# Splitting each streamed weight tile with one ScalarE copy and one DVE subtraction over 1024 columns in place of two of each

## The chip, the cores and the metric

The kernel runs on one core of one Trainium2 chip. The metric is the device time of that core in microseconds (us). Before the change it is 2222.72 us, the median of three runs (2221.65 to 2224.61).

## What is computed

The kernel computes one layer of a decoder block on 256 tokens (S) of width 2048 (D), all in fp32. Cut to what matters:

```python
def reference(x, w_in, ..., w_branch_da, w_branch_nsa, w_out, ..., peer_wq, ..., peer_u, peer_v, ...):
    ... = split_columns(x @ w_in[l])                  # one combined projection
    o_da = diff_attention(...)                        # 8 heads
    o_nsa = nsa_attention(...)                        # compressed + selected + window
    mixed = (sigmoid(g_da_merge) * (o_da @ w_branch_da[l])
             + sigmoid(g_nsa_merge) * (o_nsa @ w_branch_nsa[l]))
    h = layer_norm(DN_ALPHA * x + mixed @ w_out[l], ...)
    x = layer_norm(DN_ALPHA * h + peer_ffn(h, peer_wq[l], ..., peer_u[l], peer_v[l]), ...)
```

`peer_ffn` forms queries `y @ w_q`, picks 16 of 128 x 128 experts for each of 8 heads by two sub-key scores, and sums `gate * gelu(u[e] . y) * v[e]` over the chosen experts. `u` and `v` have 16384 rows of 2048 values each.

## The kernel before, in words

All weights are read once from HBM, as tiles of 128 x 1024 fp32 values (512 KB), in the order in which they are used: the columns of `w_in` group by group (`CHUNKS`), the two branch weights, `w_out`, `w_q`, then all rows of `u` and all rows of `v`. The experts are not gathered: the kernel multiplies `y` with every row of `u`, keeps the scores that were picked, and multiplies the sparse result `G` with every row of `v`.

**The split.** To keep nearly fp32 accuracy, each operand is split in two rounded parts, `hi` (the value rounded to the type fp32r) and `lo` (the value minus `hi`, rounded to that type again), and each product is made of three matmuls: hi times hi, lo times hi, hi times lo. The activations are split once (`xhi`, `xlo`, later `yhi`, `ylo`, and `whi`, `wlo` for `G`). A weight tile is split when it has landed, by class `Stream` (L52 to L127): `load_to` (L74) has SP issue the load into one of three buffers named `raw`; `split_upto` (L83) has ScalarE copy a half of 512 columns into `hi` (L98) and DVE subtract it from the raw half into `lo` (L99), then does the same with the other half. There are six buffers of 512 columns for each of `hi` and `lo`, so three tiles' worth. A job of another kind ("dest", L105 and L106) writes its parts into memory of its own, with one copy and one subtraction of up to 1024 columns.

**The order.** The schedule is by hand: every engine runs its instructions in the order in which the program writes them. `step` (L156) takes the split tile of its turn, runs what earlier steps had deferred, may run some background work (attention, the pick of the experts, norms), then splits the tiles up to two ahead and issues the loads behind them (`ahead`, L118; `load_ahead`, L122), and at last writes the matmuls of its own tile. So on ScalarE and DVE the split of tile i+2 stands behind the background work of step i and ahead of that of step i+1.

**How the halves are read.** `mm_T` (L193; weights stay in the array, the 256 tokens move) and `mm_N` (L204; tokens stay, 512 weight columns move) use the first half of a tile for all its matmuls and then the second. The loop over `u` (L1235 to L1261) and the loop over `v` (L1341 to L1359, with `v_mm` at L1328) use both halves from the first matmuls on. All matmuls stand in line L191. A tile is 24 matmuls of 256 columns, or 12 of 512.

**Places that the prediction speaks of.**
- In the last groups of `w_in` `W.share` is set (L804) until the first branch product (L864): there the second half's subtraction goes to GpSimd.
- The product with `w_out` (L903 to L918) holds the last tiles in buffers of their own, so that it can be finished for tokens 0 to 127 first.
- `norm` (L928; four DVE instructions in L933) normalises half of the tokens, `y_trans` (L940) transposes them on TensorE, `y_parts` (L949) makes `yhi` and `ylo`. Ahead of this, L976 has GpSimd split the first tiles of `w_q`, for the query product that follows.
- At about 740 to 765 us GpSimd works on the rows of `h` (16 instructions at L1037) and stores them to HBM (`h_d`, L1038). Later `G` takes over the memory of that tile; the loop over `u` writes it (L1251).
- `pick` (L1103) finds the experts with long DVE instructions (`eq`, L1107; `eid`, L1111), as background work of the loop over `u`.

Of the kernel before, what the change touches and what calls it, by code (L numbers as in the profile page):

```python
# [9 lines left out]
F32 = mybir.dt.float32  # L10
F32R = mybir.dt.float32r
# [5 lines left out]
OP = mybir.AluOpType  # L17
# [7 lines left out]
HALF = 1024  # L25
# [22 lines left out]
def dap(t, offset, ap):  # L48
    return bass.AP(tensor=t.tensor, offset=t.offset + offset, ap=ap)


class Stream:  # L52
# [30 lines left out]
    def split_upto(self, n, sub=None):  # L83
        sub = sub or self.nc.vector
        while self.split_to < min(n, len(self.jobs), self.cap or n):
            i = self.split_to
            self.load_to(i + 1)
            _, width, kind, dest, _, skew = self.jobs[i]
            raw = self.raw.pop(i)
            if kind == "split":  # L90
                his, los = [], []
                nb = 1 if width <= 512 else 2
                w = width // nb
                for b in range(nb):
                    hi = self.pool.tile([128, 512], F32R, name="hi", bufs=self.nsplit)
                    lo = self.pool.tile([128, 640], F32R, name="lo", bufs=self.nsplit)[:, skew:skew + 512]
                    r = raw[:, b * w:b * w + w]
                    self.nc.scalar.copy(hi[:, :w], r)  # L98
                    (self.nc.gpsimd if self.share and b else sub).tensor_tensor(lo[:, :w], r, hi[:, :w].bitcast(F32), op=OP.subtract)  # L99
                    his.append(hi[:, :w])  # L100
                    los.append(lo[:, :w])
                self.parts[i] = (his, los)
            elif kind == "dest":
                hv, lv = dest()
                self.nc.scalar.copy(hv, raw[:, :width])  # L105
                sub.tensor_tensor(lv, raw[:, :width], hv.bitcast(F32), op=OP.subtract)  # L106
                self.parts[i] = None
            else:
                self.parts[i] = (raw,)
            self.split_to += 1  # L110
# [20 lines left out]
def block_kernel(ctx, tc, x, xT, w_in, rel_bias, onehot, lamq, lamk, subln_g, pe, w1, w2k, w2v, cmask,  # L131
                 wbda, wbnsa, wout, ln1_gT, ln1_bT, ln1_g, ln1_b, wq, subk, u, v, ln2_g, ln2_b, out):
    nc = tc.nc
# [4 lines left out]
    stream = ctx.enter_context(tc.tile_pool(name="stream", bufs=3))  # L138
# [1 line left out]
    psctx = ExitStack()  # L140
    ps = psctx.enter_context(tc.tile_pool(name="ps", bufs=1, space=PSUM))

    W = Stream(nc, stream, 3, 6)

    deferred = []
    late = []
# [3 lines left out]
    def flush(every=False):  # L150
        for q in (deferred, late) if every else (deferred,):
            for f in q:
                f()
            q.clear()

    def step(fn, credit=1.0):  # L156
        part = W.take()
        flush()
        now, late[:] = list(late), []
        state["c"] = min(state["c"] + credit, 2.0)  # L160
        post = None
        while credit and slots and state["c"] > 0 and post is None:
            cost, pre, post = slots.pop(0)
            state["c"] -= cost
            if pre:
                pre()
        for f in now:
            f()
        W.ahead()
        fn(*(part or ()))  # L170
        if post:
            post()
# [75 lines left out]
    def x_job(k, n):  # L248
        W.add(dap(xT, k * S, [[KT * S, 128], [1, n * S]]), n * S, "dest",
              lambda: [t[:, k:k + n, :].rearrange("p a b -> p (a b)") for t in (xhi, xlo)],  # L250
              xraw[:, k * S:(k + n) * S])
        plan.append(("x", None, 0, 0, n // 4))
# [4 lines left out]
    for name, form, width in CHUNKS:  # L257
        for j in range(8):
            W.skew = SKEW if form == "T" else 0
            if off == 0:  # L260
                for b in range(2):
                    x_job(b, 1)
                    W.add(dap(w_in, 512 * b, [[1024, 128], [1, 512]]), 512)
                    plan.append((name, form, width, 0, b))
                x_job(2, 2)
            else:
                if name == "qd0" and j % 2 == 0:
                    x_job(2 * j, 4)
                W.add(dap(w_in, off, [[2 * width, 128], [1, 2 * width]]), 2 * width)
                plan.append((name, form, width, j, 0))  # L270
# [509 lines left out]
    for name, form, width, j, half in plan:  # L780
# [27 lines left out]
        if form == "T":  # L808
            def fn(hi, lo, j=j, half=half):
                if j == 0 and half == 0:  # L810
                    acc["b"] = [bank("acc", 4) for _ in range(2)]
                mm_T(acc["b"], hi, lo, xhi, xlo, 2 * j + half, 15)
# [67 lines left out]
    for q in range(2):  # L880
        for t in range(2):
            c = slice(HALF * q, HALF * q + HALF)
# [621 lines left out]
```

## Time and profile before

| what | value |
|---|---|
| median of three runs | 2222.72 us (2221.65 to 2224.61) |
| the profiled execution's own time | 2224.97 us |
| its span | 2223.2 us |
| TensorE matmuls busy | 2184.4 us, 98% of the span |
| DVE busy | 1452.2 us, 65% |
| ScalarE busy | 1130.3 us, 51% |
| GpSimd busy | 246.5 us, 11% |
| subtractions of 512 columns on DVE (L99) | 1390, 965.6 us |
| copies of 512 columns on ScalarE (L98) | 1462, 860.3 us |

The span runs from the first to the last recorded instruction; 1.8 us of the execution's own time lie around it. An engine's busy time counts each stretch in which it works once; PE is TensorE's matmuls, PEld its weight loads, ACT is ScalarE, POOL is GpSimd, SP issues most DMAs. In a group of instructions the mean is that of one instruction alone, so the sum of the means can be more than the busy time when neighbours overlap. Idle time is put down to what ended it.

### The profile page before, as it was taken

The page shows a single profiled execution, that of the slowest core. Times are in us where ns is not written, and L with a number is a line of the kernel's source. Part 1 is how long each engine was busy: PE and PEld are TensorE (multiplying, and loading weights), DVE is VectorE, ACT ScalarE, POOL GpSimd, SP SyncE. Part 2 cuts the span into 40 slices and gives each one's busy share as a digit, 9 for nine tenths or more (in the row PEclk, how much of TensorE's full clock was granted, in tenths as well). Part 3 has the DMA queues.
Part 4 walks back from the last instruction along what each step waited for, and adds up shares of the span by engine and source line. Part 5 has one row for each costly group of instructions (what it writes and reads, how often), then busy time and mean ns, then how long its engine had stood idle before and what let it go on. Part 6 is the DMA issues. An engine that isn't in the chain of part 4 may idle for free.

```text
span 2223.2 us, 40705 instructions
## 1 busy us (share of the span) xinstructions
PE 2184.4 (98%) x15712; PEld 2016.0 (91%) x15712; DVE 1452.2 (65%) x2898; ACT 1130.3 (51%) x2153; POOL 246.5 (11%) x223
## 2 busy tenths in 40 slices
PE   9999999999999999999999999999999999999997
PEld 9988999999987999999999999998888888888786
DVE  5558774665767889988886555555555555555567
ACT  5555654665545444455554444445555455554443
POOL 2002234443001501210000000000000000000002
PEclk9999999999999999999999999999999999999999
DMA  7664564545675766555656666666666666667774
GB/s 243 195 186 155 173 198 130 166 151 162 202 226 160 238 183 189 181 185 181 182 183 190 196 194 194 193 197 206 196 191 194 193 193 196 192 197 236 253 220 143
DMA packets 119843, 424.72 MB, mean 191 GB/s; under 512 B 13876, under 2 KB 14212, under 8 KB 119392
## 3 DMA queue, kind: packets, MB, share of 16 engines
q1 hardware_dynamic: 111600, 398.90, 58.0%
q0 software_dynamic: 5600, 18.75, 2.8%
q10 hardware_dynamic: 2448, 4.46, 0.5%
q8 instruction: 123, 2.02, 0.4%
q14 instruction: 72, 0.59, 0.1%
HBM read 413.37 MB, written 8.69 MB: 190 GB/s over the span
## 4 chain that ended last, share of the span: by engine, by line
PE 75%; DVE 8%; DMA 5%; ACT 2%; issue 2%; POOL 1%; ACTq 0%; DVEq 0%; POOLq 0%; SPq 0%
PE acc L191 43%; PE o L191 27%; DVE lo L99 4%; PE lg L191 2%; DMA raw<-in_v_dram 2%; DMA raw<-in_w_in_dram 1%; PE pv L191 1%; DMA raw<-in_wout_dram 1%; DMA raw<-in_wq_dram 1%; ACT hi L98 1%; PE tp L539 1%; DVE eq L1107 0%; DVE eid L1111 0%; DVE st L901 0%; DVE r L933 0%
## 5 line engine op out<-in xcount | busy, mean ns | idle before, releaser
L99 DVE TENSOR_TENSOR lo<-raw,hi 128x512 fp32r<-128x512 f32 (+1 forms) x1422 | 980.8, 719 | 551.2 <-ACT hi L98 549.2
L98 ACT CAST hi<-raw 128x512 fp32r<-128x512 f32 (+1 forms) x1494 | 872.4, 617 | 692.5 <-PE o L191 267.6
L191 PE MATMUL acc<-yhi,lo 128*128 128x256 f32 x2112 | 586.7, 278 | 5.5 <-DVE lo L99 5.5
L191 PE MATMUL acc<-yhi,hi 128*128 128x256 f32 x2112 | 591.4, 280 | 0.0
L191 PE MATMUL acc<-ylo,hi 128*128 128x256 f32 x2112 | 584.1, 277 | 0.0
L191 PEld LDWEIGHTS acc<-yhi,lo 128*128 128x128 f32 x2112 | 397.0, 188 | 9.4 <-DVE lo L99 9.1
L191 PEld LDWEIGHTS acc<-yhi,hi 128*128 128x128 f32 x2112 | 396.8, 188 | 0.4 <-ACT hi L98 0.2
L191 PEld LDWEIGHTS acc<-ylo,hi 128*128 128x128 f32 x2112 | 396.7, 188 | 0.0
L191 PE MATMUL o<-lo,whi 128*128 128x512 f32 x1000 | 389.7, 390 | 0.8 <-DVE lo L99 0.8
L191 PE MATMUL o<-hi,whi 128*128 128x512 f32 x1000 | 389.4, 389 | 0.6 <-ACT hi L98 0.5
L191 PE MATMUL o<-hi,wlo 128*128 128x512 f32 x1000 | 389.1, 389 | 0.0
L191 PE MATMUL acc<-xhi,hi 128*128 128x256 f32 x1024 | 290.7, 284 | 4.2 <-ACT hi L98 4.2
L191 PE MATMUL acc<-xhi,lo 128*128 128x256 f32 x1024 | 286.5, 280 | 5.5 <-DVE lo L99 5.3
L191 PE MATMUL acc<-xlo,hi 128*128 128x256 f32 x1024 | 285.2, 279 | 0.0
L191 PEld LDWEIGHTS o<-lo,whi 128*128 128x128 f32 x1000 | 187.7, 188 | 42.0 <-DVE lo L99 3.1
L191 PEld LDWEIGHTS o<-hi,whi 128*128 128x128 f32 x1000 | 187.7, 188 | 40.9 <-ACT hi L98 1.5
L191 PEld LDWEIGHTS o<-hi,wlo 128*128 128x128 f32 x1000 | 187.7, 188 | 38.5
L191 PEld LDWEIGHTS acc<-xhi,lo 128*128 128x128 f32 x1024 | 194.1, 190 | 7.8 <-DVE lo L99 7.7
L191 PEld LDWEIGHTS acc<-xhi,hi 128*128 128x128 f32 x1024 | 194.4, 190 | 6.0 <-ACT hi L98 5.6
L191 PEld LDWEIGHTS acc<-xlo,hi 128*128 128x128 f32 x1024 | 193.9, 189 | 0.0
L1282 POOL DMA_DIRECT2D back<-act_d x17 | 9.3, 546 | 1170.5 <-DVE G L1290 607.4
L99 POOL TENSOR_TENSOR lo<-raw,hi 128x512 fp32r<-128x512 f32 x72 | 104.1, 1450 | 231.7 <-ACT hi L98 228.0
(308 smaller groups left out, 2170.3 us busy)
## 6 DMA issues: line engine op xcount, KB each, us to landing
raw<-in_u_dram SPq DMA_DIRECT2D x256, 512.0 KB, 4.1
raw<-in_v_dram SPq DMA_DIRECT2D x256, 512.0 KB, 3.6
raw<-in_w_in_dram SPq DMA_DIRECT2D x143, 512.0 KB, 4.1
raw<-in_wout_dram SPq DMA_DIRECT2D x32, 512.0 KB, 4.2
raw<-in_wbda_dram SPq DMA_DIRECT2D x16, 512.0 KB, 3.9
raw<-in_wbnsa_dram SPq DMA_DIRECT2D x16, 512.0 KB, 3.8
raw<-in_wq_dram SPq DMA_DIRECT2D x16, 512.0 KB, 4.2
raw<-in_w_in_dram SPq DMA_DIRECT2D x16, 280.0 KB, 3.0
```

Source lines behind the costliest of these rows:

```text
L98: self.nc.scalar.copy(hi[:, :w], r)
L99: (self.nc.gpsimd if self.share and b else sub).tensor_tensor(lo[:, :w], r, hi[:, :w].bitcast(F32), op=OP.subtract)
L191: PE.matmul(o, a, b, start=start, stop=stop, skip_group_check=True)
L539: PE.transpose(tp[:, 128 * b:128 * b + 128], P[:, 128 * b:128 * b + 128], ident)
L1282: GP.dma_start(t, act_d[vorder[n]])
```

## The change

A tile's `hi` and `lo` become one buffer of 1024 columns each (`lo` with 128 columns more, as before, for an offset), and there are three of them in place of six of 512. One ScalarE copy writes all of `hi` and one subtraction all of `lo`. Where `W.share` is set, the two halves still have an instruction each, the first on DVE and the second on GpSimd, now into the halves of one buffer. The matmuls read the same columns in the same order. A tile of 560 columns (two halves of 280) is split in one piece too.

```diff
@@ -88,18 +88,14 @@
             _, width, kind, dest, _, skew = self.jobs[i]
             raw = self.raw.pop(i)
             if kind == "split":
-                his, los = [], []
-                nb = 1 if width <= 512 else 2
-                w = width // nb
-                for b in range(nb):
-                    hi = self.pool.tile([128, 512], F32R, name="hi", bufs=self.nsplit)
-                    lo = self.pool.tile([128, 640], F32R, name="lo", bufs=self.nsplit)[:, skew:skew + 512]
-                    r = raw[:, b * w:b * w + w]
-                    self.nc.scalar.copy(hi[:, :w], r)
-                    (self.nc.gpsimd if self.share and b else sub).tensor_tensor(lo[:, :w], r, hi[:, :w].bitcast(F32), op=OP.subtract)
-                    his.append(hi[:, :w])
-                    los.append(lo[:, :w])
-                self.parts[i] = (his, los)
+                hi = self.pool.tile([128, HALF], F32R, name="hi", bufs=self.nsplit)
+                lo = self.pool.tile([128, HALF + 128], F32R, name="lo", bufs=self.nsplit)[:, skew:skew + HALF]
+                w = width if width <= 512 else width // 2
+                cuts = [slice(c, c + w) for c in range(0, width, w)]
+                for e, c in zip((sub, self.nc.gpsimd), cuts) if self.share else ((sub, slice(0, width)),):
+                    self.nc.scalar.copy(hi[:, c], raw[:, c])
+                    e.tensor_tensor(lo[:, c], raw[:, c], hi[:, c].bitcast(F32), op=OP.subtract)
+                self.parts[i] = ([hi[:, c] for c in cuts], [lo[:, c] for c in cuts])
             elif kind == "dest":
                 hv, lv = dest()
                 self.nc.scalar.copy(hv, raw[:, :width])
@@ -140,7 +136,7 @@
-    W = Stream(nc, stream, 3, 6)
+    W = Stream(nc, stream, 3, 3)
```

`HALF` is 1024. In the changed kernel the lines behind the edit stand four lower, and L98, L99, L106 become L96, L97, L102.

At the start of the program, ScalarE (`xhi<-gn` is the split of a part of the tokens, `hi<-raw` that of a weight tile; the first weight tile of `w_in` comes as two loads of 512 columns, which the rows ahead of these split). Before:

```order
L105 CAST xhi<-gn 128x512
L98 CAST hi<-raw 128x512 x2
L105 CAST xhi<-gn 128x1024
L98 CAST hi<-raw 128x512 x4
L105 CAST xhi<-gn 128x1024
L98 CAST hi<-raw 128x512 x4
```

After the change:

```order
L101 CAST xhi<-gn 128x512
L96 CAST hi<-raw 128x1024
L101 CAST xhi<-gn 128x1024
L96 CAST hi<-raw 128x1024 x2
L101 CAST xhi<-gn 128x1024
L96 CAST hi<-raw 128x1024 x2
```

Each pair of copies of a tile has become one; their places in the row are the same.

GpSimd, from the loads of the norm's parameters to the query product (the rows `lo<-raw,hi` are those of L976, `gn<-raw,gn` is a held tile of `w_q`). Before:

```order
L895 DMA g1T_8495<-in_ln1_gT_dram 128x16
L896 DMA b1T_8496<-in_ln1_bT_dram 128x16
L883 DMA gd_8481<-in_x_dram 128x1024 x4
L99 TENSOR_TENSOR lo_9174<-raw_9069,hi_9173 128x512
L99 TENSOR_TENSOR lo_9178<-raw_9069,hi_9177 128x512
L99 TENSOR_TENSOR lo_9182<-raw_9085,hi_9181 128x512
L99 TENSOR_TENSOR lo_9186<-raw_9085,hi_9185 128x512
L106 TENSOR_TENSOR gn_8494<-raw_9101,gn_8494 128x1024
```

After the change:

```order
L891 DMA g1T_7827<-in_ln1_gT_dram 128x16
L892 DMA b1T_7828<-in_ln1_bT_dram 128x16
L879 DMA gd_7813<-in_x_dram 128x1024 x4
L97 TENSOR_TENSOR lo_8406<-raw_8309,hi_8405 128x1024
L97 TENSOR_TENSOR lo_8410<-raw_8321,hi_8409 128x1024
L102 TENSOR_TENSOR gn_7826<-raw_8333,gn_7826 128x1024
```

Four subtractions of 512 columns have become two of 1024; the third tile's, of 1024 columns, was in one piece already.

DVE, in the pick of the experts (`eq` and `eid` are that pick's instructions, `lo<-raw,hi` are subtractions for tiles of `u`). Before:

```order
L1107 TENSOR_TENSOR eq_11441<-iota_9411,posf_9425 128x800
L1111 TENSOR_REDUCE eid_9426<-eq_11370 128x16
L99 TENSOR_TENSOR lo_11446<-raw_11341,hi_11445 128x512
L99 TENSOR_TENSOR lo_11450<-raw_11341,hi_11449 128x512
L1107 TENSOR_TENSOR eq_11479<-iota_9411,posf_9425 128x800
L1111 TENSOR_REDUCE eid_9426<-eq_11441 128x16
L99 TENSOR_TENSOR lo_11484<-raw_11381,hi_11483 128x512
L99 TENSOR_TENSOR lo_11488<-raw_11381,hi_11487 128x512
L99 TENSOR_TENSOR lo_11520<-raw_11415,hi_11519 128x512
L99 TENSOR_TENSOR lo_11524<-raw_11415,hi_11523 128x512
```

After the change:

```order
L1103 TENSOR_TENSOR eq_10457<-iota_8627,posf_8641 128x800
L1107 TENSOR_REDUCE eid_8642<-eq_10394 128x16
L97 TENSOR_TENSOR lo_10462<-raw_10365,hi_10461 128x1024
L1103 TENSOR_TENSOR eq_10491<-iota_8627,posf_8641 128x800
L1107 TENSOR_REDUCE eid_8642<-eq_10457 128x16
L97 TENSOR_TENSOR lo_10496<-raw_10401,hi_10495 128x1024
L97 TENSOR_TENSOR lo_10528<-raw_10431,hi_10527 128x1024
```

The subtractions stand between the same instructions of the pick, one where there were two.

## Rows read from the trace of the kernel before

**Rows 1.** The page's busy time, share of the span and instructions of each engine.

```profile
PE 2184.4 (98%) x15712; PEld 2016.0 (91%) x15712; DVE 1452.2 (65%) x2898; ACT 1130.3 (51%) x2153; POOL 246.5 (11%) x223
```

**Rows 2.** TensorE's waits: what was waited for, us in total, times, longest.

```profile
PE acc L191 <- DVE lo L99: 11.0, 19, 1.4
...
PE acc L191 <- ACT hi L98: 4.2, 3, 2.4
...
PE acc L191 <- ACT yhi L964: 1.5, 1, 1.5
```

**Rows 3.** Stretches: busy us (xinstructions) of each engine, clock, DMA share, GB/s.

```profile
185.00:266.00 81.00, 74.47 (x628) 71.48 (x628) 63.23 (x136) 47.74 (x111) 21.11 (x19) 1.00 0.54 171
736.00:772.00 36.00, 35.60 (x290) 34.55 (x289) 34.52 (x55) 17.70 (x33) 25.27 (x17) 1.00 0.71 234
850.00:970.00 120.00, 116.23 (x991) 113.57 (x990) 112.57 (x277) 56.13 (x100) 29.28 (x17) 1.00 0.57 179
1200.00:1500.00 300.00, 300.00 (x2650) 300.00 (x2649) 159.18 (x249) 139.09 (x249) 0.00 (x0) 1.00 0.65 194
```

**Rows 4.** Start, in order of time: start, length, engine, instructions, [idle before, releaser].

```profile
11.62 1.14 ACT L98 CAST hi<-raw 128x512 fp32r<-128x512 f32 x2 [0.86 <-DMA raw<-in_w_in_dram]
12.27 1.29 DVE L99 TENSOR_TENSOR lo<-raw,hi 128x512 fp32r<-128x512 f32 x2 [0.79 <-ACT hi L98]
13.02 0.39 PE L191 MATMUL acc<-xhi,lo 128*128 128x256 f32 x1 [0.34 <-DVE lo L99]
```

**Rows 5.** Start of the product with `w_out`, in order of time, TensorE.

```profile
630.40 0.50 PE L191 MATMUL acc<-lo,xhi 128*128 128x512 f32 x1 [0.23 <-DVE lo L99]
```

**Rows 6.** Norm and query product, in order of time, the engines apart.

```profile
697.37 4.81 DVE L933 TENSOR_SCALAR r<-r,mv,rstd 128x512 f32<-128x512 f32 x4
...
712.98 1.92 DVE L933 TENSOR_SCALAR r<-r,mv,rstd 128x512 f32<-128x512 f32 x4
...
697.73 5.59 POOL L99 TENSOR_TENSOR lo<-raw,hi 128x512 fp32r<-128x512 f32 x4 [75.74 <-ACT hi L98]
...
735.62 0.39 PE L191 MATMUL acc<-yhi,lo 128*128 128x256 f32 x1 [1.33 <-DVE lo L99]
```

**Rows 7.** The loop over `v`, in order of time, TensorE.

```profile
2068.45 0.50 PE L191 MATMUL o<-lo,whi 128*128 128x512 f32 x1 [0.23 <-DVE lo L99]
```

**Rows 8.** The second-last tile of `v`, in order of time.

```profile
2194.64 1.14 ACT L98 CAST hi<-raw 128x512 fp32r<-128x512 f32 x2 [1.35 <-DMA raw<-in_v_dram]
...
2196.09 0.45 PE L191 MATMUL o<-lo,whi 128*128 128x512 f32 x1
```

**Rows 9.** Groups by line and shape: xcount | busy, mean ns | idle before, releaser.

```profile
L99 DVE TENSOR_TENSOR lo<-raw,hi 128x512 fp32r<-128x512 f32 x1390 | 965.6, 724 | 540.9 <-ACT hi L98 538.9
L98 ACT CAST hi<-raw 128x512 fp32r<-128x512 f32 x1462 | 860.3, 621 | 683.5 <-PE o L191 267.6 <-PE acc L191 165.3 <-DVE lo L99 69.7
...
L106 DVE TENSOR_TENSOR vl<-raw,vh 128x1024 fp32r<-128x1024 f32 x6 | 7.4, 1226 | 5.3 <-ACT vh L105 5.2
L105 ACT CAST vh<-raw 128x1024 fp32r<-128x1024 f32 x6 | 6.3, 1049 | 6.0 <-DMA raw<-in_v_dram 6.0
...
L106 POOL TENSOR_TENSOR gn<-raw,gn 128x1024 fp32r<-128x1024 f32 x1 | 2.4, 2407 | 0.0
```

**Rows 10.** The rows of `h`, in order of time; its store's us to landing; ScalarE.

```profile
738.95 27.48 DVE L99 TENSOR_TENSOR lo<-raw,hi 128x512 fp32r<-128x512 f32 x18 [1.22 <-ACT hi L98]
...
764.37 0.59 POOL L1038 DMA_DIRECT2D h_d<-r  x1 [0.30 <-POOL r L1037]
...
h_d<-r POOLq DMA_DIRECT2D x2, 1024.0 KB, 5.8
...
775.01 1.28 ACT L1251 ACT_TABLE_LOAD   x1 [0.72 <-issue]
```

**Rows 11.** Groups by line and shape of TensorE, products with `y` and `x`.

```profile
L191 PE MATMUL acc<-yhi,hi 128*128 128x256 f32 x2112 | 591.4, 280 | 0.0
...
L191 PE MATMUL acc<-xhi,hi 128*128 128x256 f32 x1024 | 290.7, 284 | 4.2 <-ACT hi L98 4.2
```

## The prediction

> **What bounds the kernel now.** I read the busy shares first: TensorE is busy for 98% of the span [rows 1]. An edit to the split of weight tiles is therefore worth nothing by the work it saves on ScalarE or DVE; it is worth what it adds to or takes from the stalls of TensorE. The list of TensorE's waits gives the stock: 11.0 us in 19 waits for a `lo` half and 4.2 us in 3 waits for a `hi` half [rows 2]; its other waits for a split are under 1 us each. About 15 us, 0.7% of the time, is all that a better split could win.
>
> The stretches then show where a split can be late [rows 3]. From 1200 to 1500 us (the scores against `u`) TensorE is busy 300.00 of 300 us with DVE at half load: a tile of 24 matmuls takes 24 x 300/2650 = 2.72 us, and the next tiles are always ready. From 736 to 772 and from 850 to 970 us DVE is busy 34.5 of 36 and 112.6 of 120 us, and TensorE has holes of 0.4 and 3.8 us: here the split is late because DVE is full. From 185 to 266 us (the differential attention) the holes are 6.5 of 81 us, and DVE, with 63 us of work, is full in bursts. At a third kind of place it is late because the load is: ScalarE sat idle until the raw tile landed, and TensorE takes the first half the moment it is there [rows 4 to 8].
>
> **The change part by part.** *Fewer instructions.* The built program has 1314 rows on ScalarE in place of 2060, and 1917 on DVE in place of 2593. By the mean durations a tile would save 2 x 621 - 1049 = 193 ns on ScalarE and 2 x 724 - 1226 = 222 ns on DVE [rows 9]. I do not take these: two casts in a row last 1.14 us together and two subtractions 1.29 us [rows 4], so neighbours overlap, and one of 1024 columns lasts 1.05 and 1.23 us [rows 9]. The engines really win 0.09 and 0.06 us a tile. On TensorE's path that is zero wherever DVE has room; it counts only in the DVE-full stretches.
>
> *A coarser first half.* Now TensorE can start a tile once half of it is cast and subtracted, 0.62 + 0.69 = 1.31 us after the landing (by their means 0.62 and 0.72, [rows 9]). Afterwards it needs the whole of both, 1.05 + 1.23 = 2.28 us. Where the landing is the cause of the lateness, the first matmul on `lo` comes 0.97 us later by these means; I take 0.95. Where DVE's queue is the cause, only the subtraction is longer, 1.23 for 0.69, so 0.5 us; in the `u` stage both halves are used from the first matmuls on, the second was ready after 1.29 us anyway, and little is lost (I take 0.2 us).
>
> *Buffers released as whole tiles.* Three buffers of 1024 columns hold what six of 512 held. A matmul that reads half after half (`mm_T`, `mm_N`) freed the first half 1.36 us earlier than the second; this is lost. `u` and `v` read both halves to the end of a tile, so nothing changes there. What hides the loss is the depth of two tiles: a split that starts when tile i-1 is done has 2 x 2.72 = 5.44 us until tile i+2 is needed, and takes 2.28. If that cover were gone, a tile would wait up to 1.36 us; it is gone where DVE runs a burst of over 3.1 us, which happens in the differential attention (185 to 266 us), where I put the loss inside that stretch's sum.
>
> *Loads.* SP issues the same loads in the same order. A raw tile is free when its last subtraction ends: 2.28 us after the landing in place of 0.62 + 0.03 + 1.29 = 1.94, so a load that is limited by buffers starts up to 0.34 us later.
>
> *ScalarE/DVE/GpSimd sharing* (from `g0` to the first branch product) keeps two halves with an instruction each; I take zero, and the bounds hold 0.5 us either way.
>
> Now the sum, place by place.
> - Start: the raw tile lands at 11.62 and TensorE takes `lo` at 13.02 [rows 4]. That tile took 1.40, so 0.88 would be added by its own rows, 0.97 by the means: plus 0.95. Bounds 0, if a later load is the true limit, and 1.36, a half tile; the tile's own rows are nearest.
> - `w_out`: the same at 630.40 [rows 5], plus 0.95.
> - GpSimd splits two tiles for the query product while DVE normalises: four subtractions of 5.59 us in all on GpSimd, and four DVE instructions that need 4.81 us, until 702.18 [rows 6]. In place of four subtractions there will be two of 2.41 us (the row of 1024 columns on GpSimd, [rows 9]). DVE gets two of its four through before GpSimd starts and one after each of the two, so its last comes at about 703.2 for 702.2: plus 1.0 on the transposes. TensorE then waits 1.5 us for `yhi` at 715 us in any case [rows 2], and that chain was held by GpSimd's end, which does not move. Sum zero, bounds 0 and 1.9.
> - Query product: TensorE waited 1.33 us for `lo` until 735.62, with GpSimd at work beside DVE [rows 6]; DVE is the cause, so the longer subtraction counts, 1.23 - 0.69: plus 0.6.
> - Last `v` tiles: 2068.45 is again landing-bound [rows 7], plus 0.95, and 0.3 more as later loads start later; the second-last tile lands at 2194.64 and its `lo` is taken at 2196.09 [rows 8]; afterwards it is there at 2194.64 + 2.28 + 0.03 = 2196.95, plus 0.85.
> - Gains. From 738.95 us, 18 half subtractions take 27.48 us while GpSimd works on the rows of `h` [rows 10]: 3.05 us a tile, slower than TensorE's 2.72. One subtraction per tile meets GpSimd once in place of twice, 1.23 plus the 0.85 us by which these 18 exceed their plain length (27.48/18 = 1.53, less 0.68, the middle of 1.29/2 and 0.72), some 2.1 us: below 2.72, so the holes there go. Nine tiles x 0.33 = 3.0 us is the bound; part of it was lead, I take half, minus 1.5. From 850 to 970 us 991 matmuls are 41 tiles: 41 x 0.06 = 2.5 us of DVE's time, less 0.2 for the last coarse tile, minus 2.3; bounds 0 and the 3.8 us that are there. From 185 to 266 us the holes are 6.5, not all for a split; 25 tiles save 25 x 0.06 = 1.5 and a GpSimd instruction is met half as often, but each late `lo` there grows by up to 0.5: minus 0.5, bounds -3 and +2.
>
> Losses 0.95 + 0.95 + 0.6 + 1.25 + 0.85 = 4.6, gains 1.5 + 2.3 + 0.5 = 4.3: plus 0.3 us. The profiled execution took 2224.97 us and would take 2225.3; it lies 2.2 us above the median of the three runs, 2222.72, so the forecast median is 2223.0.
>
> **A rule weighed.** The rows of the norm [rows 6] show DVE and GpSimd in each other's way: the same four DVE instructions last 1.92 us where GpSimd is idle and 4.81 beside its subtractions, one turn of GpSimd for each after the first. [...]
>
> **The rivals.**
> 1. *DVE's relief is all that counts* (faster). If the DVE-full stretches lose all that is there, 3.8 from 850 to 970 us, the bound of 3.0 from 736 to 772 and half of the 6.5 from 185 to 266, that is 10.0 against losses of 4.6: minus 5.4, 2217.3. For it: DVE at 94% there. Against: only 2.5 us of DVE time is really saved in 120. [...]
> 2. *The coarse half wins* (slower). It decides where a tile's subtraction starts within 0.95 us of its use. If all 19 waits for `lo` grow by 0.5 us and nothing returns, that is 9.5, and the five landing-bound places add the other 0.45 each, 2.2: 11.7, 2234. If only the landing-bound ones grow and the gains fail, 4.6: 2227.3. For it: five such places stand in the rows. Against: in the DVE-full stretches the end is set by DVE's total.
> 3. *GpSimd becomes late* (slower). It issues the store of `h` at 764.37, landing 5.8 us later, 770.2; ScalarE first writes `G` over that memory after 775.0 [rows 10]. That is 4.8 us of room. If each of GpSimd's 16 instructions waits a whole longer subtraction (0.54 more), it is 8.6 us late, 3.8 too much, and the casts queue behind ScalarE's wait: 2226.8 with my sum.
> 4. *The addresses matter*, and the stream change is not what decides. The diff moves no other tile itself, but it shifts the memory behind the stream's: six halves took 6 x (2048 + 2560) = 27,648 bytes a partition, three tiles take 3 x (4096 + 4608) = 26,112, and whatever is allocated behind lies 1,536 bytes lower. The matmuls on `x` and on `y`, which lie at different places, last 284 and 280 ns [rows 11]. If the 3,072 on `x` moved by such 4 ns, it would be 12 us either way, 2211 or 2235. Against: `y` does not move, and `hi` and `lo` keep their distances within 512 bytes.
>
> **How the numbers follow.** No measurable change 0.66. Rival 1: 0.13; rival 2: 0.12, of which most at the smaller price; rival 3: 0.04; rival 4: 0.02 faster, 0.03 slower. The line is drawn at 0.2%, 4.4 us, which is what I call no change: 2218.3 to 2227.1, about what a measurement of this kernel can tell from it. That gives faster 0.15, same 0.66, slower 0.19. The range reaches over the same band and into the smaller price of rival 2 and the near side of rival 1: 2217.5 to 2229.
>
> **What would show it.** Right: DVE's `lo` instruction at 1.2 us, no `lo` wait of TensorE between 738 and 772 us, the wait at 13.0 us grown to 13.9, waits near 2068 and 2196 us grown by 0.9, and 850 to 970 us with 1 to 3 us less of waits. Wrong: waits for `hi` or `lo` in the stretch from 1200 to 2040 us, where I have none; a matmul of 256 columns that no longer takes 113 ns; or a sum of waits for `lo` outside 8 to 18 us.

## The result, and the profile after

The changed kernel takes 2239.31 us (median of six runs, 2236.01 to 2240.48) against 2223.75 us before (median of six, 2221.65 to 2224.76): a ratio of 1.0069, 95% interval 1.0058 to 1.0080. It is 15.6 us slower; 2223.0 was forecast, with a range up to 2229. The profiled execution took 2240.48 us, its span is 2238.6 us.

The changed kernel's page, busy time of each engine [rows 1]:

```profile
PE 2188.7 (98%) x15712; PEld 2019.1 (90%) x15712; DVE 1369.9 (61%) x2222; ACT 1042.6 (47%) x1475; POOL 249.2 (11%) x221
```

DVE has 82 us less to do and ScalarE 88, and the program is longer: what these engines have to do in total did not set the time. TensorE's waits in the changed kernel [rows 2]:

```profile
PE acc L187 <- DVE lo L97: 16.8, 24, 1.8
PE acc L187 <- ACT hi L96: 5.0, 5, 1.9
PE o L187 <- DVE lo L97: 4.6, 8, 0.8
PE pv L941 <- DVE r L929: 1.8, 1, 1.8
PE acc L187 <- DVE hl L102: 1.4, 1, 1.4
...
PE o L187 <- ACT hi L96: 1.1, 2, 0.6
...
PE acc L187 <- ACT yhi L960: 1.1, 1, 1.1
```

The waits of `acc` for `lo` grew from 11.0 to 16.8 us, those of `o` for `lo` (the loop over `v`) from 0.8 to 4.6 us, and that of the last transposes of the norm (`pv`) from 0.8 to 1.8 us. Before:

```profile
PE o L191 <- DVE lo L99: 0.8, 4, 0.2
...
PE pv L945 <- DVE r L933: 0.8, 1, 0.8
```

The stretches of [rows 3] in the changed kernel:

```profile
185.00:266.00 81.00, 72.66 (x589) 69.87 (x588) 57.64 (x109) 43.18 (x80) 18.67 (x18) 0.96 0.53 164
736.00:772.00 36.00, 35.48 (x261) 33.40 (x260) 17.39 (x12) 15.35 (x19) 26.70 (x19) 1.00 0.81 276
850.00:970.00 120.00, 115.60 (x1007) 114.42 (x1006) 111.99 (x261) 52.56 (x58) 29.12 (x16) 1.00 0.59 183
1200.00:1500.00 300.00, 300.00 (x2650) 300.00 (x2649) 155.56 (x139) 129.76 (x139) 0.00 (x0) 1.00 0.65 195
```

From 1200 to 1500 us nothing changed: 2650 matmuls in 300 us. The first stretch lost clock too: the granted clock is 0.96 where it was 1.00. The stretches are cut by each run's own time; by 736 us the changed kernel is some 9 us behind, so that its second and third rows show earlier work than the rows before.

TensorE runs the same 15712 matmuls in the same order in every kernel here, so the time between the starts of the same two matmuls can be compared from trace to trace. In us, with the stretches named by their time before, and three kernels of the experiments beside them ("two of each" has two copies and two subtractions a tile, "one of each" one, "four raw" a fourth load buffer; the first row begins with the first matmul, the last ends with the start of the last):

| stretch | before | changed | two of each, whole buffers | two of each, four raw | one of each, four raw |
|---|---|---|---|---|---|
| start to 60 | 58.7 | 59.2 | 57.5 | 59.0 | 58.3 |
| 185 to 212, attention | 27.1 | 31.1 | 30.2 | 29.0 | 30.8 |
| 212 to 400, attention | 188.0 | 188.5 | 186.9 | 186.0 | 185.2 |
| 600 to 640, `w_out` starts | 40.1 | 41.0 | 40.1 | 39.2 | 39.2 |
| 685 to 738, norm and query | 52.9 | 55.6 | 52.8 | 49.5 | 50.8 |
| 738 to 970, `h` rows and pick | 232.0 | 232.4 | 232.2 | 232.3 | 232.2 |
| 970 to 2040, `u` and `v` | 1070.1 | 1070.1 | 1070.1 | 1070.2 | 1070.1 |
| 2040 to 2100, `v` with other loads | 59.9 | 63.8 | 60.6 | 56.4 | 56.4 |
| 2190 to the end, last tiles of `v` | 19.3 | 22.2 | 19.7 | 19.0 | 19.0 |

(The stretches left out hold 460.1 to 460.3 us in every column.) The loss of the changed kernel is 4.6 us in the attention (4.0 and 0.6), 2.7 at the norm, 3.9 and 2.9 in the loop over `v`, 0.9 at `w_out`; behind the last matmul it gets 0.7 us back (13.1 us in place of 13.8).

How a late place looks now. In order of time, the start of `w_out`, of the query product's norm, and the last tiles of `v` in the changed kernel [rows 5, 6, 8]:

```profile
634.38 1.05 ACT L96 CAST hi<-raw 128x1024 fp32r<-128x1024 f32 x1 [6.38 <-DMA raw<-in_wout_dram]
635.46 1.23 DVE L97 TENSOR_TENSOR lo<-raw,hi 128x1024 fp32r<-128x1024 f32 x1 [6.20 <-ACT hi L96]
635.48 0.49 PE L187 MATMUL acc<-hi,xhi 128*128 128x512 f32 x1 [0.45 <-ACT hi L96]
636.74 0.50 PE L187 MATMUL acc<-lo,xhi 128*128 128x512 f32 x1 [0.77 <-DVE lo L97]
...
705.10 6.01 DVE L929 TENSOR_SCALAR r<-r,mv,rstd 128x512 f32<-128x512 f32 x4
...
705.95 4.88 POOL L97 TENSOR_TENSOR lo<-raw,hi 128x1024 fp32r<-128x1024 f32 x2 [78.48 <-ACT hi L96]
...
711.17 1.11 PE L941 MATMUL pv<-ident,r 128*128 128x128 f32 x4 [1.83 <-DVE r L929]
...
2210.95 0.50 PE L187 MATMUL o<-hi,whi 128*128 128x512 f32 x1 [0.48 <-ACT hi L96]
...
2212.21 0.50 PE L187 MATMUL o<-lo,whi 128*128 128x512 f32 x1 [0.76 <-DVE lo L97]
```

At `w_out` the matmul on `lo` starts 636.74 - 634.38 = 2.36 us after the copy began; before it was 630.40 - 629.00 = 1.40, with the copy in this row:

```profile
629.00 1.14 ACT L98 CAST hi<-raw 128x512 fp32r<-128x512 f32 x2 [6.80 <-DMA raw<-in_wout_dram]
```

The one wait of 0.23 us has become two, 0.45 for `hi` and 0.77 for `lo`. At the norm the four DVE instructions take 6.01 us in place of 4.81 and the last transposes wait 1.83 us for them. The loop over `v` from 2064 to 2098 us, TensorE [rows 7]:

```profile
2067.13 0.49 PE L187 MATMUL o<-hi,whi 128*128 128x512 f32 x1 [0.63 <-ACT hi L96]
2068.39 0.50 PE L187 MATMUL o<-lo,whi 128*128 128x512 f32 x1 [0.77 <-DVE lo L97]
...
2071.85 0.50 PE L187 MATMUL o<-lo,whi 128*128 128x512 f32 x1 [0.45 <-DVE lo L97]
...
2081.46 0.50 PE L187 MATMUL o<-lo,whi 128*128 128x512 f32 x1 [0.76 <-DVE lo L97]
...
2084.92 0.50 PE L187 MATMUL o<-lo,whi 128*128 128x512 f32 x1 [0.43 <-DVE lo L97]
...
2094.09 0.49 PE L187 MATMUL o<-lo,whi 128*128 128x512 f32 x1 [0.69 <-DVE lo L97]
...
2097.55 0.50 PE L187 MATMUL o<-lo,whi 128*128 128x512 f32 x1 [0.43 <-DVE lo L97]
```

It is not one late tile but three rounds of them, each with a wait at its first tile and another at the next. What ties the rounds together is the raw buffer: SP issues the next load when the split has released it. The first split of a round with the load behind it, in the kernel before and in the changed one:

```profile
2054.78 1.14 ACT L98 CAST hi<-raw 128x512 fp32r<-128x512 f32 x2 [5.77 <-DMA raw<-in_v_dram]
2055.43 1.29 DVE L99 TENSOR_TENSOR lo<-raw,hi 128x512 fp32r<-128x512 f32 x2 [5.70 <-ACT hi L98]
2056.75 0.33 SPq L79 DMA_DIRECT2D raw<-in_v_dram  x1
```

```profile
2066.03 1.05 ACT L96 CAST hi<-raw 128x1024 fp32r<-128x1024 f32 x1 [6.54 <-DMA raw<-in_v_dram]
2067.11 1.23 DVE L97 TENSOR_TENSOR lo<-raw,hi 128x1024 fp32r<-128x1024 f32 x1 [6.36 <-ACT hi L96]
2068.36 0.33 SPq L79 DMA_DIRECT2D raw<-in_v_dram  x1
```

In both the load is issued 0.03 us after the subtraction's end. From the copy's start to the load it takes 2068.36 - 2066.03 = 2.33 us in place of 2056.75 - 2054.78 = 1.97.

### The profile page after: what moved, and what is told of

The parts are those of the page before. It is cut to its first block, busy times and chain, and to the rows that moved or that the text cites. A ratio compares the mean times of both kernels' runs of the same rounds, so it can differ in the third digit from the quotient of the medians.

```text
span 2238.6 us, 38793 instructions
## 1 busy us (share of the span) xinstructions
PE 2188.7 (98%) x15712; PEld 2019.1 (90%) x15712; DVE 1369.9 (61%) x2222; ACT 1042.6 (47%) x1475; POOL 249.2 (11%) x221
## 4 chain that ended last, share of the span: by engine, by line
PE 77%; DVE 7%; DMA 4%; ACT 2%; issue 1%; POOL 0%; ACTq 0%; DVEq 0%; POOLq 0%
PE acc L187 46%; PE o L187 27%; DVE lo L97 3%; PE lg L187 2%; DMA raw<-in_v_dram 2%; ACT hi L96 1%; DMA raw<-in_wout_dram 1%; PE pv L187 1%; PE tp L535 1%; DVE st L897 0%; DVE eq L1103 0%; ACT P L508 0%; DVE r L929 0%; DVE eid L1107 0%; DVE hb L896 0%
## 5 line engine op out<-in xcount | busy, mean ns | idle before, releaser
L97 DVE TENSOR_TENSOR lo<-raw,hi 128x1024 fp32r<-128x1024 f32 (+2 forms) x746 | 892.3, 1200 | 686.4 <-ACT hi L96 679.0
L96 ACT CAST hi<-raw 128x1024 fp32r<-128x1024 f32 (+2 forms) x816 | 784.0, 971 | 783.7 <-PE acc L187 319.5
L97 POOL TENSOR_TENSOR lo<-raw,hi 128x512 fp32r<-128x512 f32 (+1 forms) x70 | 103.4, 1479 | 234.3 <-ACT hi L96 197.9
```

The source lines that it names most:

```text
L96: self.nc.scalar.copy(hi[:, c], raw[:, c])
L97: e.tensor_tensor(lo[:, c], raw[:, c], hi[:, c].bitcast(F32), op=OP.subtract)
```

## The experiments

**Two of each, with a shorter lead.** Theory 1 was that the longer instructions cost the time at places that are late anyway; theory 2 that the buffers of whole tiles, or the addresses, do. The first four kernels put the two copies and two subtractions back, in part or in quarters. The edit of the first:

```diff
-                for e, c in zip((sub, self.nc.gpsimd), cuts) if self.share else ((sub, slice(0, width)),):
+                for n, c in enumerate(cuts):
+                    e = self.nc.gpsimd if self.share and n else sub
                     self.nc.scalar.copy(hi[:, c], raw[:, c])
```

The others do the copy or the subtraction in one piece, or both in four. All four have an effect that was not meant: `n` is also the bound of the loop over tiles, so a call splits no second tile, and tiles are split later than before.

> Buffers of whole tiles as in the changed kernel, but two copies and two subtractions a tile as before. If the longer instructions cost the 15.6 us (theory 1: a late tile comes later in one piece, and its raw buffer is released later): 2221 to 2227 us, and the clock stays up from 185 to 330 us. If the buffers that are released as whole tiles, or the 1,536 bytes by which the memory behind them moved, cost it (theory 2): 2233 to 2240. A split between them, say 2229 to 2232, would give both a part.

> One copy of 1024 columns, two subtractions of 512. The first half of lo is ready 1.05 + 0.69 = 1.74 us after the landing (before 1.31, changed 2.28), the raw buffer is free after 1.05 + 0.03 + 1.29 = 2.37 (before 1.94, changed 2.28). Theory 1, if the first half decides: 2228 to 2233; if the release of the raw buffer decides: 2236 to 2242. Theory 2: like the changed kernel, 2236 to 2241.

> Two copies of 512 columns, one subtraction of 1024. Both the first half of lo and the release of the raw buffer come 1.14 + 0.03 + 1.23 = 2.40 us after the landing, 0.12 later than in the changed kernel. Theory 1, either way: 2238 to 2244, not better than the changed kernel although ScalarE's part is undone. Theory 2: 2236 to 2241. If ScalarE's long copy were the cause: below 2232.

> Four copies and four subtractions of 256 columns, in buffers of whole tiles. Estimates from 0.62 and 1.05 us for 512 and 1024 columns (0.40 for 256) and from 0.69 and 1.23 (0.42): the first quarter of lo is ready 0.85 us after the landing, the whole tile after some 1.85 (before 1.31 and 1.94). Theory 1: the places that wait for a landing gain 0.1 to 0.5 us each against two of each, DVE needs some 1.40 us a tile in place of 1.29 where it is full: within 4 us of the run with two of each, on either side. Theory 2: equal to the run with two of each within 1.5 us.

Measured: 2255.21 us (ratio 1.0146, 1.0131 to 1.0162), 2282.77 (1.0271, 1.0257 to 1.0285), 2311.70 (1.0398, 1.0382 to 1.0413) and 2256.84 (1.0153, 1.0139 to 1.0167). The first three expectations missed. The fourth, to be within 4 us of the run with two of each, was met (1.6 us), but holds for the shorter lead alone. TensorE's waits for `lo` in the first of them:

```profile
PE acc L188 <- DVE lo L98: 22.5, 33, 2.0
```

By the same two matmuls, its loss lies between 738 and 2040 us, where it takes 28 us more than the kernel before; the last stretches are like before. These runs say nothing on the two theories. They show what the lead is worth: with the splits as far ahead as before the same instructions take 2228.60 us, 26.6 us less.

**Two of each, one copy, one subtraction, and `u` alone.** The same with the loop over tiles as it was:

```diff
-                for e, c in zip((sub, self.nc.gpsimd), cuts) if self.share else ((sub, slice(0, width)),):
+                for e, c in zip((sub, self.nc.gpsimd if self.share else sub), cuts):
```

For one copy, `hi[:, :width]` is written ahead of this loop; for one subtraction, `lo[:, :width]` behind it. For `u` alone a set of tile numbers chooses one or two of each.

> Buffers of whole tiles, two copies and two subtractions a tile, and the splits as far ahead as before (in the four runs named e the loop over tiles ended after one tile a call, because the edit used its bound's name again; they show what a shorter lead costs, not the instruction's length). Theory 1, the long instructions at places that are late anyway: 2221 to 2227 us. Theory 2, buffers released as whole tiles or the shifted addresses: 2233 to 2240.

> One copy of 1024 columns, two subtractions of 512, the lead as before. First half of lo 1.74 us after a landing (before 1.31, changed 2.28), raw buffer free after 2.37 (before 1.94, changed 2.28). Theory 1, if the first half decides: 2228 to 2233; if the release of the raw buffer decides: 2236 to 2242. Theory 2: like the changed kernel, 2236 to 2241.

> Two copies of 512 columns, one subtraction of 1024, the lead as before. First half of lo and release of the raw buffer both 2.40 us after a landing (changed 2.28 for both). Theory 1: 2238 to 2244, no better than the changed kernel. Theory 2: 2236 to 2241. If ScalarE's long copy is the cause: 2222 to 2232.

> One copy and one subtraction for the tiles of u alone (256 of 479), two of each elsewhere, buffers of whole tiles. In the changed kernel's trace TensorE lost 0.3 us or less between 772 and 2040 us. Theory 1: within 2 us of the run with two of each, although 256 tiles have the long instructions, as these tiles are split ahead of need. If the length cost something on every tile: a good half of the 15.6 us, 2230 or more.

Measured: 2228.60 us (1.0021, 1.0009 to 1.0032), 2237.03 (1.0062, 1.0048 to 1.0076), 2244.92 (1.0100, 1.0085 to 1.0116) and 2227.37 (1.0017, 1.0008 to 1.0026). Two of each came out 1.6 us above the range of theory 1 and 4.4 us below that of theory 2, one copy in the range for the release of the raw buffer, one subtraction 0.9 us above its range, and `u` alone as expected. So the long instructions cost 2239.3 - 2228.6 = 10.7 us and the rest of the edit some 5. By the sums in the expectations (estimates from the lengths of the instructions in the trace of before) the first half of `lo` is ready 1.31, 1.74, 2.28 and 2.40 us after a landing with two of each, one copy, the changed kernel and one subtraction (the changed kernel's rows above have 2.31 from the copy's start to the subtraction's end), and the times stand in that order: 2228.6, 2237.0, 2239.3 and 2244.9. By the end of the whole split (1.94, 2.37, 2.28 and 2.40 us) the one copy is 2.3 us out of order. But neither gives a price: the first 0.43 us of lateness cost 8.4 us, the next 0.54 us only 2.3, the last 0.12 us 5.6. Both count, and how much each has is not shown. Undoing ScalarE's part alone made it worse, as theory 1 says. And 256 of 479 tiles, those of `u`, can have the long instructions at no cost that shows.

The start of `w_out` with one copy, in order of time:

```profile
633.17 0.50 PE L190 MATMUL acc<-hi,xhi 128*128 128x512 f32 x1 [1.93 <-ACT hi L96]
...
633.90 0.50 PE L190 MATMUL acc<-lo,xhi 128*128 128x512 f32 x1 [0.22 <-DVE lo L100]
```

Here the matmul on `lo` waits 0.22 us, as before the change, and the one ahead of it 1.93 us for `hi`. The copy is only 0.43 us longer; the rest is a later landing. So two things grow with the split: the piece, and the time at which the next load could start (here 2.44 us after the start of the copy, 1.98 in the kernel before).

**One stage at a time.** Long instructions for the tiles before 600 us alone, and for those of `v` alone.

> One copy and one subtraction for the tiles of w_in, of the compression weights and of the two branch weights alone (before 600 us), two of each elsewhere, buffers of whole tiles. By the traces of the changed kernel and of two of each in whole buffers (2228.6 us) this part takes 4 us more with long instructions, half of it at a lower clock: 2230 to 2234 us. If the loss lies in the tiles of u and v: 2227 to 2230.

> The same for the tiles of v alone. Of 256 tiles some ten wait for a landing, three of them in a row while other transfers take the DMA engines (2040 to 2100 us), the others at the end. By those traces 3.2 + 2.4 us: 2232 to 2236 us. If those losses are chance of the one profile: 2227 to 2230.

Measured: 2231.68 us (1.0035, 1.0021 to 1.0049) and 2231.30 (1.0031, 1.0019 to 1.0043), 3.1 and 2.7 us above two of each; the first as expected, the second a little under. Both intervals overlap that of two of each, so neither difference is clear of the noise by itself; together they would be 5.8 of the 10.7 us. In its trace the run with `v` alone takes 63.8 us from 2040 to 2100 and 22.0 from 2190 on, the values of the changed kernel to 0.2 us. For the first of the two that is in part luck: 3.4 us of this stretch ran at a lower clock in this run (0.97 in the mean from 2040 to 2100 us) and none in the changed kernel (1.00), and the holes are 3.5 us against 4.6. The tiles of `w_out` and `w_q` were not tried alone.

**Addresses.** 384 unused columns behind the stream's buffers, with two of each:

```diff
     W = Stream(nc, stream, 3, 3)
+    stream.tile([128, 384], F32, name="pad", bufs=1)
```

> Two of each in whole buffers, and 384 unused columns behind the stream's buffers, so that all memory behind them lies where it lay before the change. If the addresses cost the 5 us: 2221 to 2225 us. If the buffers that are released as whole tiles cost them: 2227 to 2231. In both cases the length of a matmul's turn stays as it is.

Measured: 2228.13 us (1.0018, 1.0009 to 1.0027), as expected, like two of each without it. The shifted memory costs nothing that shows; by elimination the 5 us belong to the buffers that are released as whole tiles, which no run shows by itself. The traces place them only in part. Here is the stretch between the matmuls that start at 185 and at 212 us before, in order in the kernel before, two of each, the changed kernel, and the run `k3_raw4_halves` from below, which has half buffers:

```profile
185.04:212.10 27.06, 23.49 (x193) 22.01 (x192) 23.49 (x44) 13.37 (x32) 12.68 (x13) 1.00 0.39 111
```

```profile
183.87:214.06 30.19, 26.30 (x194) 24.75 (x192) 26.10 (x52) 16.32 (x39) 12.64 (x13) 0.89 0.44 133
```

```profile
185.58:216.63 31.05, 26.16 (x193) 24.86 (x192) 26.17 (x46) 16.04 (x31) 12.25 (x13) 0.89 0.44 135
```

```profile
187.79:217.04 29.25, 26.46 (x193) 24.81 (x192) 25.15 (x51) 15.45 (x37) 12.62 (x13) 0.88 0.44 126
```

TensorE's holes (length less busy time) are 3.6, 3.9, 4.9 and 2.8 us. Its matmuls are busy 23.5 us before and 26.2 to 26.5 in the others, where the granted clock was 0.50 in place of 1.00 for 6.8 us from between 206 and 209 us on. So two of each lose 0.3 us here to waits and 2.8 to the clock, the changed kernel 1.3 and 2.7. The fall goes neither with whole buffers, as the last row shows, nor with the holes alone: the run with one copy has 5.2 us of them at a clock of 1.00. And it is not the 5 us: the mean clock of all runs is 0.9958 before, 0.9955 in two of each, the padded run and `u` alone, and 0.9938 in the changed kernel, which over some 2230 us is worth under 1 us and some 4 us at most (an estimate, as if matmuls filled that time). Over the whole attention, 185 to 400 us, two of each have fewer holes than the kernel before (9.3 us, 10.7 before), and the changed kernel's 2.5 us more than two of each are holes (12.3 us) at equal clock. What else the trace of two of each shows are waits that grow by 0.9 us at 691 us (`hl`, a held tile), and 0.7 and 0.4 us in the two stretches of `v`; its whole span is only 2.1 us longer than that of the kernel before.

**A fourth raw buffer.** If the split's length acts through the raw buffers, a fourth should take that part away.

```diff
-SKEW = 96
+SKEW = 48
...
-                lo = self.pool.tile([128, HALF + 128], F32R, name="lo", bufs=self.nsplit)[:, skew:skew + HALF]
+                lo = self.pool.tile([128, HALF + 48], F32R, name="lo", bufs=self.nsplit)[:, skew:skew + HALF]
...
-    W = Stream(nc, stream, 3, 3)
+    W = Stream(nc, stream, 4, 3)
```

> Whole buffers, two copies and two subtractions, and four raw buffers in place of three, so that a load does not wait for the split of the tile three before it but four; the offset of lo is 48 columns in place of 96 to make room. If the raw buffers tie the late landings to the length of a split: the waits at 630, 2040 to 2100 and 2196 us shrink by 1 us or more in all, 2222 to 2227. If the DMA engines alone set those landings: 2227 to 2230. The offset of 48 could cost something of its own.

> The changed kernel (one copy and one subtraction) with four raw buffers and the offset of 48. If the release of the raw buffer carries the loss: most of the 10.7 us between two of each and one of each goes, 2226 to 2231. If the late piece itself (lo in one piece, 2.28 us after a landing) carries it: 2234 to 2240.

Measured: 2253.50 us (1.0132, 1.0116 to 1.0149) and 2257.83 (1.0157, 1.0142 to 1.0172): both far above what was expected. From 1200 to 1500 us, the first of them:

```profile
1200.00:1500.00 300.00, 300.00 (x2576) 299.96 (x2574) 154.43 (x241) 136.37 (x245) 0.00 (x0) 1.00 0.64 188
```

TensorE does 2576 matmuls where it did 2650, with no hole and at full clock: every one is slower by 2.9%. What changed there beside the fourth buffer is the place of `lo`. The next kernels keep the old offset and find the room otherwise: the `lo` buffers in one tile at distances of 4096 bytes, with two of each, one of each, and the halves of before.

```diff
-                lo = self.pool.tile([128, HALF + 128], F32R, name="lo", bufs=self.nsplit)[:, skew:skew + HALF]
+                c0 = HALF * (self.turn % self.nsplit) + skew
+                self.turn += 1
+                lo = self.los[:, c0:c0 + HALF]
```

> Two of each in whole buffers, four raw buffers, the lo buffers in one tile at multiples of 4096 bytes with the old offset of 96 columns. With the turns of the matmuls as before, the stalls that the earlier run with four raw buffers lost (32.6 to 20.4 us) should show: 2213 to 2219 us. If the slower matmuls of that run came from the fourth buffer and not from the offset: 2250 again.

> One of each, four raw buffers, lo as in the run before. If the release of the raw buffer carries the loss of the changed kernel: within 3 us of the run with two of each and four raw buffers. If the late piece itself carries it: 8 to 11 us above that run. The earlier pair (slowed by the offset) differed by 4.3, so 3 to 6 us above it: 2217 to 2224.

> The kernel before (six half buffers, two of each) with four raw buffers and the lo buffers in one tile, which makes room for the fourth. Against two of each in whole buffers it has the hi halves released apart: 0 to 4 us less than that run, 2210 to 2217 us, faster than both kernels. If the raw buffers had not bound anything before: 2221 to 2225.

Measured: 2226.36 us (1.0013, 1.0004 to 1.0022), 2236.88 (1.0057, 1.0043 to 1.0071) and 2222.18 (0.9989, 0.9980 to 0.9998). All three were expected lower (2213 to 2219, 2217 to 2224 and 2210 to 2217). The first two are 27.1 and 21.0 us faster than the pair with the offset of 48 columns, with as many raw buffers; and with four raw buffers and `lo` as in the changed kernel the stretch from 970 to 2040 us takes 1070.2 us, 1070.1 before (the table above). So the slow matmuls went with the place of the buffers and not with their number. But a tile with offset 96 now overlaps its neighbour with offset 0 by 96 columns, and where the offset changes TensorE gets new waits (17.5 us for `lo`, 10.5 in two of each) and a lower clock (0.9939 in the mean of its runs, 0.9953 in two of each): the first of the three takes 3.6, 4.6 and 6.8 us longer than two of each from 120 to 160, 280 to 300 and 720 to 740 us. The last pair avoids that: `lo` as in the changed kernel, room from the one-hot rows.

```diff
-        one, ob = [gs["oh"].tile([128, 4, 128, 2], F16, name=x, bufs=n) for x, n in (("one", 2), ("ob", 3))]
+        one, ob = [gs["oh"].tile([128, 4, 128, 2], F16, name=x, bufs=n) for x, n in (("one", 2), ("ob", 2))]
...
-    W = Stream(nc, stream, 3, 3)
+    W = Stream(nc, stream, 4, 3)
```

> Two of each in whole buffers, four raw buffers, two buffers of one-hot rows in place of three. If the waits at the three places hung on the raw buffers, and the new waits of the earlier pair on the lo tile: 2215 to 2221 us, faster than both kernels. If two buffers of one-hot rows hold DVE up between 970 and 1200 us: up to 5 us more.

> The same with one of each. If the late release of a raw buffer were all of the loss: within 2 us of the run with two of each. As the attention, the start and the norm lose by the late piece itself (some 6 of the 10.5 us between the earlier pair): 5 to 9 us above it, 2221 to 2229, and equal to it from 2040 us on.

Measured: 2214.17 us (0.9960, 0.9947 to 0.9974) and 2219.11 (0.9981, 0.9972 to 0.9990). Both are faster than the kernel before, the first by 9 us, and just below their expected ranges; at the three places the extra waits of the earlier pair are gone (in all, 8.6 and 14.2 us for `lo` in place of 17.5 and 23.2). The long instructions still cost 4.9 us, in place of 10.7. The buffer of one-hot rows that made the room was not taken away by itself. From 2040 to 2100 us, in order the kernel before, the changed kernel, and these two:

```profile
2040.00:2100.00 60.00, 58.54 (x251) 46.42 (x250) 31.91 (x51) 27.58 (x49) 5.86 (x11) 1.00 0.77 264
```

```profile
2040.00:2100.00 60.00, 55.38 (x234) 43.02 (x234) 29.13 (x29) 21.83 (x24) 6.92 (x13) 1.00 0.74 254
```

```profile
2040.00:2100.00 60.00, 60.00 (x266) 49.70 (x265) 35.06 (x56) 29.64 (x53) 6.38 (x12) 1.00 0.86 273
```

```profile
2040.00:2100.00 60.00, 60.00 (x266) 49.69 (x265) 34.85 (x35) 27.78 (x30) 6.40 (x12) 1.00 0.83 275
```

With three raw buffers TensorE has holes and the DMA engines are busy for 0.74 to 0.77 of the time; with a fourth they are busy for 0.83 to 0.86 and TensorE for all of it, with long instructions or short. At `w_out`, here and at the end the two kernels are equal to 0.1 us (the table above): there the length of a split acts only where the loads cannot run further ahead. In the attention and at the norm the difference stays, 1.0 and 1.4 us in these two traces; they are of executions only 1.9 us apart (2216.66 and 2218.56 us), so the rest of the 4.9 us is not placed.

## Why the prediction was wrong

The mechanism of rival 2, the coarse half, had 0.12. Even its larger price, 2234, is below what was measured. The sum of the waits for `lo`, 16.8 + 4.6 = 21.4 us, lies outside the 8 to 18 us that were to tell a wrong prediction. Four steps failed: the attention (4.6 us measured, a gain of 0.5 in the sum), the loads of `v` (6.8 for 2.1), the gains from DVE's relief (0.4 lost, 3.8 gained in the sum) and the norm with the query product (2.7 for 0.6). By the terms of the sum, each against the same two matmuls:

- *Start, plus 0.95*: the piece is right (12.87 - 10.52 = 2.35 us from copy to `lo`, before 1.40), in this execution the tile landed 1.1 us earlier: plus 0.5.

```profile
10.52 1.04 ACT L96 CAST hi<-raw 128x1024 fp32r<-128x1024 f32 x1 [0.64 <-DMA raw<-in_w_in_dram]
...
12.87 0.58 PE L187 MATMUL acc<-xhi,lo 128*128 128x256 f32 x1 [0.68 <-DVE lo L97]
```

- *`w_out`, plus 0.95*: plus 0.9, right.
- *Norm and query product, 0 and plus 0.6*: plus 2.7 together. DVE's four instructions took 1.2 us more, as forecast (1.0). That this was covered by the later wait for `yhi` was wrong: that wait shrank by 0.4 us only, the transposes waited 2.9 us (before 1.5), a held tile of `w_out` came 1.0 us later (0.9 with two of each), and the granted clock from 706 to 716 us was 0.83. On the other side the wait of 1.33 us for `lo` went away in place of growing; an earlier one of 0.5 came. Of the 2.7 us, 1.2 are holes and 1.6 slower matmuls. In the trace the two DVE instructions beside GpSimd's subtractions, of 2.4 and 2.5 us, last 2.6 us each, and the two ahead of them 0.5.
- *Last `v` tiles, 1.25 and 0.85*: plus 3.9 and 2.9. This is the largest step that failed in the sum of losses: "a load that is limited by buffers starts up to 0.34 us later" has the right size (0.36 by the rows above) but was priced once, at 0.3, like the one late tile. With three raw buffers the whole split stands between a landing and the next load; from 2040 to 2100 us that is paid in each of three rounds, and again at the end. The runs with a fourth buffer show it: there one and two of each are equal (56.4 and 19.0 us both).
- *Attention, minus 0.5*: plus 4.6. About 2 of it come with two of each in whole buffers, in that trace by the lower clock (2.8 us from 185 to 212 us); the other 2.5 are waits. The loss of "the first half 1.36 us earlier" was put inside a sum and then netted to a gain. The fall of the clock had no term at all.
- *The gains at 738 and 850 us, minus 1.5 and 2.3*: plus 0.4 from 738 to 970 us. DVE's relief is real, but hardly reaches TensorE (from 850 to 970 us, by the same matmuls, 119.7 us in place of 120.0). The groups on DVE in the pick, before (850 to 970 us):

```profile
L99 DVE TENSOR_TENSOR lo<-raw,hi 128x512 fp32r<-128x512 f32 x82 | 66.3, 860 | 2.8 <-ACT hi L98 2.7
L1107 DVE TENSOR_TENSOR eq<-iota,posf 128x800 f32<-128x800 f32 x16 | 15.7, 981 | 0.1
```

  and in the changed kernel (860 to 980 us, the same work):

```profile
L97 DVE TENSOR_TENSOR lo<-raw,hi 128x1024 fp32r<-128x1024 f32 x41 | 62.0, 1530 | 4.2 <-ACT hi L96 4.1
L1103 DVE TENSOR_TENSOR eq<-iota,posf 128x800 f32<-128x800 f32 x16 | 17.3, 1079 | 0.1
```

  `lo` saves 4.3 us of DVE, `eq` loses 1.6 of them (one of the 16 lasts 2.56 us, beside an instruction of 2.62 us on GpSimd, the others 0.98), and each late tile waits for a piece of 1.23 us in place of 0.69.

Right were: nothing between 970 and 2040 us, no cost of the addresses (rival 4), GpSimd never late (rival 3), and the 0.95 us of one late tile. Wrong was to set 4.3 us of saved engine time against 4.6 us of lateness. What stays open: how the whole buffers cost 5 us, how the 10.7 us divide between the later piece and the later load, and why the clock falls at some 207 us in some kernels and not in others.

## What to carry to other kernels

A piece that is on the path only when it is late is priced by its latency, and here busy time saved on an engine that is not the bound set almost nothing against that. Follow the buffer too: when its release gates the next load, the longer piece is paid in every round that is late, not once (here three rounds, 3.9 us). Here one more load buffer (with one buffer of one-hot rows fewer) was worth 14 us with two of each and 20 with one of each, more than any choice of the split.

## What was not expected of the hardware

With `lo` at an offset of 48 columns, in buffers of 4288 bytes a partition, each matmul of the loop over `u` took 300/2576 in place of 300/2650 us, 116.5 for 113.2 ns, at full clock and without a hole. With the buffers at distances of 4096 bytes and the offset of 96, the run with the same instructions took 27.1 us less (2226.36 for 2253.50). The loop over `v` has no offset and is slower in that run too, 91.2 us for 90.0 between the same matmuls from 2100 to 2190 us; so the offset is not needed for it. Whether the distance of the buffers does it, or the addresses of other tiles that may move with it, was not tried.
